# First loads by k-tile, the end in smaller parts, and a smaller stock in the gated embedding

## The chip, the cores and the metric

The kernel runs on one core of a Trainium2 chip. The metric is the device time of one execution in microseconds (us). A core has several engines that run side by side and wait for each other through semaphores: TensorE (PE, matmuls, with its weight loads shown as PEld), VectorE (DVE), ScalarE (ACT), GpSimd (POOL) and SyncE (SP, which here only issues DMAs). Each engine takes its instructions in the order in which the program gives them, so an instruction that waits holds up everything behind it on its engine.

## The reference, cut to what matters

A trunk of two layers over 256 tokens with a model width of 1024. Each layer is half a SwiGLU FFN, a token mixer (latent attention in layer 0, forgetting attention in layer 1), a second half FFN, and a gated embedding. One RMSNorm ends it.

```python
    h = x
    for i in range(DEPTH):
        h = h + 0.5 * swiglu(rms_norm(h, ffn_norm[i, 0]), ffn_w_in[i, 0], ffn_w_out[i, 0])
        u = rms_norm(h, mix_norm[i])
...
        h = h + 0.5 * swiglu(rms_norm(h, ffn_norm[i, 1]), ffn_w_in[i, 1], ffn_w_out[i, 1])
        gate = jax.nn.sigmoid(rms_norm(h, ple_norm[i]) @ ple_w_gate[i])
        h = h + gate * (p[i] @ ple_w_proj[i])
    return rms_norm(h, final_norm)
```

All arrays are float32. The hidden width of the FFN is 2816.

## The kernel before

**Two-part numbers.** Every large matmul is done in the type fp32r on numbers split into a high part and a low part: high x high, low x high, high x low. For the weights, ACT writes the high part `whi` (a copy that rounds, line 98) and DVE the low part `wlo` (raw minus high, line 102). For the activations, `Norm.high` (line 269) multiplies by the gain on ACT, or on DVE where `vector=True`, and `Norm.low` (line 277) makes the rest on DVE. `part` (line 225) runs one k-tile of 128 rows: one matmul with `whi` against both parts of the activations (512 columns), one with `wlo` against the high part (256 columns).

**The stream of weights.** All weights stand in one list, `plan`, in order of use, in blocks of 128 x 1024 (512 KB). `Weights` keeps counters over it: `fetched` (DMA issued on SP into one of four `raw` buffers), `begun` (high part issued on ACT), `loaded` (low part issued on DVE) and `got` (handed to matmuls). `pump` issues high parts up to two blocks ahead, then the low part of one block, and then the next fetches. Each of these is written into the engines' order at the place where `pump` is called. `catch_up(n)` pumps one block if fewer than `n` blocks are loaded beyond `got`. `get` pumps until what it hands out is loaded.

**The start.** `xT` holds the gains (80 columns) and the residual stream by k-tile (8 x 256 columns); it goes into `state` in three pieces, alternating on SP's queue with four slabs of 128 x 1024 that hold, two k-tiles each, the weights of the first two chunks' gate and up (`ffn_first`). Two raw blocks, the tokens `xt` (for the sums of squares by token) and two further raw blocks follow. 22 matmuls on zeros warm up TensorE. Then, per k-tile, ACT and DVE make the pairs of stream and weights, and `first` runs the four products (gate and up of chunks 0 and 1) side by side, k-tile by k-tile.

**The FFN** (line 322). For each of 22 chunks of 128 hidden units, `pg` (gate) and `pu` (up) are made in PSUM from eight k-tiles each. There are seven PSUM banks under the tag "mm", taken in turn. A product leaves its bank when DVE multiplies it by `rb2` (`two`, line 329), the norm's factor per token; that factor comes from `by_token` (`v` on DVE, `rtok` on POOL) and `by_column` (`pb` on PE, `rb` on ACT), which the program issues after the first chunk that follows the waiting ones. Until `rb` is there, no bank is freed. In FFNs other than the first, `blocks` (line 253) runs the first chunk: seven k-tiles of `pg`, seven of `pu`, then the eighth of each.

**The gated embedding of layer 0**, `ple` (line 784). Two blocks of `ple_proj` and then eight of `ple_gate`, one per row d of 128 features. For each d, `gated` issues on DVE the product with `rb` (`zg`), the low part of row d-1's next norm, then weight work (`W.pump(2 - d)` for d under 2, `W.catch_up(3)` for d from 2 to 6), then the product with the gate (`ge`), and the sum into `state`. For the last row it issues `nxt.last` (high and low part on DVE) and then `W.pump()`. The next FFN's first chunk follows.

**The end**, `ple_by_token` (line 827), works with tokens on the partitions (two halves t of 128 tokens). PE makes 512 output columns for both halves, then the other 512: for t = 0 in one piece, for t = 1 in two pieces of 256. After each piece `gated` applies the sigmoid (ACT), the product and the sum (DVE), the square with its sum by token (ACT) and the product with the final gain (DVE). `store` adds the sums, takes the power -1/2 on POOL, scales, and issues the stores. The first store stands between the two last pieces.

## Time and profile before

| | us |
|---|---|
| median of 3 runs | 1001.46 |
| lowest, highest | 1001.19, 1002.36 |
| the profiled execution's own time | 1001.46 |
| its span (first to last instruction) | 999.7 |
| mean granted TensorE clock | 0.998 |

How to read the rows that follow below: a row of the timeline has the start in us from the span's start, the duration, engine, line of the kernel, operation, output <- inputs, shapes, and a count where equal neighbours are merged; in square brackets stands the idle time of that engine before the instruction, and what ended it. A row of a stretch has busy time of each engine with the number of instructions, then the granted clock, the share of the 16 DMA engines, and GB/s.

### The profile page before, as it was taken

What the parts mean: (1) busy time and instruction counts of PE and PEld (TensorE: products, weight loads), DVE (VectorE), ACT (ScalarE), POOL (GpSimd) and SP (SyncE); (2) the same over time, 40 slices, a digit from 0 to 9 for tenths busy, and PEclk for the clock granted to TensorE, in tenths of its full rate; (3) what the DMA queues carried; (4) which work ended last, traced back from release to release, by engine and by line L of the source; (5) the groups of instructions that cost most, each with busy time, mean ns of one, the idle gap of its engine ahead of it and who ended that gap; (6) DMA issues with size and microseconds to landing.
All of it is one profiled execution on the core that took longest, in us unless ns stands there. A gap on an engine that the chain in (4) does not pass through costs nothing.

```text
span 999.7 us, 16018 instructions
## 1 busy us (share of the span) xinstructions
PE 988.8 (99%) x5940; PEld 875.1 (88%) x5940; DVE 740.5 (74%) x1051; ACT 517.6 (52%) x825; POOL 423.7 (42%) x348
## 2 busy tenths in 40 slices
PE   9999999999999999999999999999999999999996
PEld 7888888998988888889888888899889888888886
DVE  5777879676768787667778876666777778876674
ACT  7555444456655544555555444546445554544552
POOL 0777730110267775111477673211221577671120
PEclk9999999999999999999999999999999999999999
DMA  8566666651456666665366656666443566666561
GB/s 330 177 209 208 190 181 191 187 169 53 132 182 207 189 190 185 193 196 195 127 198 206 192 182 192 180 194 206 151 142 102 189 202 199 189 179 201 178 210 43
DMA packets 51388, 180.54 MB, mean 181 GB/s; under 512 B 5872, under 2 KB 6000, under 8 KB 51312
## 3 DMA queue, kind: packets, MB, share of 16 engines
q1 hardware_dynamic: 50880, 178.75, 57.3%
q8 instruction: 47, 0.77, 0.3%
q10 hardware_dynamic: 432, 0.79, 0.3%
q14 instruction: 29, 0.24, 0.1%
HBM read 178.46 MB, written 1.05 MB: 180 GB/s over the span
## 4 chain that ended last, share of the span: by engine, by line
PE 91%; DVE 4%; ACT 2%; issue 1%; POOL 0%; DMA 0%; POOLq 0%; SPq 0%; ACTq 0%; DVEq 0%
PE pu L236 16%; PE po L236 16%; PE pg L236 16%; PE po L237 8%; PE pu L237 8%; PE pg L237 8%; PE ps L236 4%; PE ps L237 2%; DVE wlo L102 1%; PE ps L221 1%; PE ps L223 1%; PE ps L222 1%; PE pv L221 1%; PE pv L223 1%; PE pv L222 1%
## 5 line engine op out<-in xcount | busy, mean ns | idle before, releaser
L102 DVE TENSOR_TENSOR wlo<-raw,whi 128x1024 fp32r<-128x1024 f32 (+2 forms) x338 | 416.8, 1241 | 17.8 <-ACT whi L98 17.1
L98 ACT ACTIVATE whi<-raw 128x1024 fp32r<-128x1024 f32 (+2 forms) x338 | 336.4, 1027 | 20.9 <-DMA raw<-in_ffn_in_dram 12.9
L331 POOL TENSOR_TENSOR gu<-two 128x256 f32<-128x256 f32 x176 | 235.5, 1339 | 117.9 <-DVE two L329 108.4
L236 PE MATMUL pg<-u,whi 128*128 128x512 f32 x704 | 251.7, 395 | 0.8 <-ACT whi L98 0.4
L236 PE MATMUL pu<-u,whi 128*128 128x512 f32 x704 | 251.1, 395 | 0.0
L236 PE MATMUL po<-hs,whi 128*128 128x512 f32 x704 | 246.0, 394 | 0.0
L237 PE MATMUL pg<-u,wlo 128*128 128x256 f32 x704 | 198.2, 282 | 0.3 <-DVE wlo L102 0.2
L237 PE MATMUL po<-hs,wlo 128*128 128x256 f32 x704 | 198.1, 281 | 0.0
L237 PE MATMUL pu<-u,wlo 128*128 128x256 f32 x704 | 198.0, 281 | 0.0
L236 PEld LDWEIGHTS pg<-u,whi 128*128 128x128 f32 x704 | 132.2, 188 | 32.1 <-DVE u L280 1.3
L236 PEld LDWEIGHTS pu<-u,whi 128*128 128x128 f32 x704 | 132.2, 188 | 30.3
L236 PEld LDWEIGHTS po<-hs,whi 128*128 128x128 f32 x704 | 132.2, 188 | 30.2
L237 PEld LDWEIGHTS pg<-u,wlo 128*128 128x128 f32 x704 | 132.5, 188 | 0.9 <-DVE wlo L102 0.9
L237 PEld LDWEIGHTS pu<-u,wlo 128*128 128x128 f32 x704 | 132.5, 188 | 0.0
L237 PEld LDWEIGHTS po<-hs,wlo 128*128 128x128 f32 x704 | 132.5, 188 | 0.0
L291 POOL TENSOR_TENSOR acc<-acc,sq 128x256 f32<-128x256 f32 x42 | 46.0, 1094 | 173.7 <-ACT sq L286 173.5
L213 ACT ACTIVATE hs<-hid 128x256 fp32r<-128x256 f32 x88 | 36.8, 418 | 142.1 <-POOL hid L349 140.1
L349 POOL TENSOR_TENSOR hid<-sg,gu 128x256 f32<-128x256 f32 x88 | 105.2, 1196 | 7.0 <-POOL gu L331 0.2
L217 DVE TENSOR_TENSOR hs<-hid,hs 128x256 fp32r<-128x256 f32 x88 | 63.5, 721 | 48.6 <-ACT hs L213 48.6
L329 DVE TENSOR_TENSOR two<-pg,rb 128x512 f32<-128x512 f32 x88 | 60.3, 685 | 46.8 <-PE pg L237 38.9
L275 ACT ACTIVATE u<-state 128x256 fp32r<-128x256 f32 x57 | 29.0, 509 | 125.7 <-DVE state L392 104.3
L343 ACT ACTIVATE sg<-gu 128x256 f32<-128x256 f32 x88 | 36.8, 418 | 78.5 <-POOL gu L331 78.5
(247 smaller groups left out, 1189.2 us busy)
## 6 DMA issues: line engine op xcount, KB each, us to landing
raw<-in_ffn_in_dram SPq DMA_DIRECT2D x172, 512.0 KB, 4.1
raw<-in_ffn_out_dram SPq DMA_DIRECT2D x64, 512.0 KB, 3.6
raw<-in_ffn_out_dram SPq DMA_DIRECT2D x32, 384.0 KB, 3.7
raw<-in_fox_qk_dram SPq DMA_DIRECT2D x16, 512.0 KB, 3.5
raw<-in_mla_o_dram SPq DMA_DIRECT2D x8, 512.0 KB, 4.4
raw<-in_ple_gate_dram SPq DMA_DIRECT2D x8, 512.0 KB, 4.6
raw<-in_fox_o_dram SPq DMA_DIRECT2D x8, 512.0 KB, 3.7
raw<-in_ple_rows_dram SPq DMA_DIRECT2D x8, 512.0 KB, 4.7
```

What stands on the lines that cost most here:

```text
L98: self.nc.scalar.activation(self.pairs[i][0][:, c], self.raws[i][:, c], AF.Copy)
L102: self.nc.vector.tensor_sub(lo[:, c], self.raws[i][:, c], hi[:, c].bitcast(F32))
L213: nc.scalar.activation(hi, src, AF.Copy)
L217: nc.vector.tensor_sub(lo, src, hi.bitcast(F32))
L236: nc.tensor.matmul(ps, hi, x[:, k], start=k == 0, stop=False)
L237: nc.tensor.matmul(ps[:, 1, :], lo, x[:, k, 0, :], start=False, stop=k == last)
L275: nc.scalar.activation(self.pair[:, b, 0, c], src[:, c], AF.Copy, scale=g)
L291: nc.gpsimd.tensor_add(new, self.acc, sq)
L329: nc.vector.tensor_mul(two, ps, norm.rb2)
L331: nc.gpsimd.tensor_add(gu[c, i], two[:, 0, :], two[:, 1, :])
L343: nc.scalar.activation(sg, gu.pop((c, 0)), AF.Silu)
L349: nc.gpsimd.tensor_mul(hid[c], gu.pop((c, 0)), gu.pop((c, 1)))
```

## The change

Three places are changed.

1. *The start.* The residual stream and the first weights of one k-tile now stand in one row of DRAM per partition, 256 + 512 columns; the row of k-tile 0 has the first 16 gains ahead of it. Eight DMAs bring them. `state`, whole, is loaded by one further DMA behind the tokens and the first raw blocks. The first norm reads its gains from the lead tile and takes its stream from there. The high part of k-tile 0 is made on DVE, there are 18 warm-up matmuls, and for k-tile 0 the four matmuls with high weights come ahead of the four with low ones.
2. *The gated embedding.* `W.catch_up(2)` in place of `W.catch_up(3)` for d from 2 to 6.
3. *The end.* The last 512 columns of token half 1 are made in pieces of 256, 128 and 128, all issued on PE in one go. The sum of squares is carried along piece by piece (`mean`) instead of being reduced at the end; the product with the final gain (`weigh`) is issued apart from the rest; the last scaling is cut into 384 columns on ACT and 640 on DVE, each with its own store.

```diff
@@ -79,10 +79,9 @@
         self.fetched += 1
         return raw, src

-    def take(self, raws):
-
-        self.raws.update(enumerate(raws))
-        self.fetched = self.ahead = len(raws)
+    def skip(self, n):
+
+        self.fetched = self.ahead = n

     def fetch(self):
         while self.fetched < min(len(self.plan), max(self.ahead, self.loaded) + self.RAW):
...
@@ -155,7 +154,7 @@

     def plan_ffn(i):

-        plan.extend(ffn_first[k] for k in range(0 if i else KD // 2))
+        plan.extend(ffn_in[0, c] for c in range(0 if i else KD // 2))
         plan.extend(ffn_in[i, c] for c in range(0 if i else 4, 2 * KF))
         for d in range(KD):
             plan.extend(ffn_out[i, d, :, a * P:min(a + KD, KF) * P] for a in range(0, KF, KD))
@@ -262,12 +261,13 @@
     class Norm:


-        def __init__(self, gain, blocks, dim, tag="u"):
-            self.gain, self.dim, self.acc, self.sums = gain, dim, None, None
+        def __init__(self, gain, blocks, dim, tag="u", table=g_sb):
+            self.g = table[:, gain:gain + blocks]
+            self.dim, self.acc, self.sums = dim, None, None
             self.pair = act.tile([P, blocks, 2, T], F32R, name=tag, bufs=2 if tag == "u" else 1)

         def high(self, b, src, vector=False, cuts=(slice(0, T),)):
-            g = g_sb[:, self.gain + b:self.gain + b + 1]
+            g = self.g[:, b:b + 1]
             for c in cuts:
                 if vector:
                     nc.vector.tensor_scalar(self.pair[:, b, 0, c], src[:, c], g, None, op0=ALU.mult)
...
@@ -793,7 +793,7 @@
             if d < 2:
                 W.pump(2 - d)
             elif d < KD - 1:
-                W.catch_up(3)
+                W.catch_up(2)
             nc.vector.tensor_mul(ge, e, sg)
             nc.vector.tensor_add(src, src, ge)
             if d < KD - 1:
@@ -831,7 +831,7 @@
         nc.sync.dma_start(gain, gain_row.to_broadcast([P, D]))
         N = D // 2
         half = [slice(0, N), slice(N, D)]
-        sums = work.tile([P, 2, 3], F32, name="sums", bufs=1)
+        sums = work.tile([P, 2, 4], F32, name="sums", bufs=1)

         def rows(ps, w, x, k, a, t, last):

@@ -844,21 +844,29 @@
             nc.vector.tensor_mul(sg, es[:, t, a], sg)
             nc.vector.tensor_add(h[:, t, a], h[:, t, a], sg)
             nc.scalar.activation(sg, h[:, t, a], AF.Square, accum_out=sums[:, t, i:i + 1])
+
+        def weigh(t, a):
             nc.vector.tensor_mul(es[:, t, a], h[:, t, a], gain[:, a])

-        def store(t, n):
-            s = work.tile([P, 1], F32, name="s")
-            v = work.tile([P, 1], F32, name="v1")
-            r = work.tile([P, 1], F32, name="r")
-            nc.vector.reduce_sum(s, sums[:, t, :n], axis=AX.X)
-            nc.vector.tensor_scalar(v, s, 1.0 / D, EPS, op0=ALU.mult, op1=ALU.add)
-            nc.gpsimd.tensor_tensor(r, v, mhalf[:, :1], op=ALU.pow)
-            for i, a in enumerate(half):
-                if t and i == 0:
-                    nc.scalar.activation(h[:, t, a], es[:, t, a], AF.Copy, scale=r)
+        def mean(t, i):
+
+            v = work.tile([P, 1], F32, name="v1", bufs=4)
+            nc.vector.tensor_scalar(v, sums[:, t, i:i + 1], 1.0 / D, means[t], op0=ALU.mult, op1=ALU.add)
+            means[t] = v
+
+        def store(t, cuts):
+            for i, (eng, a) in enumerate(cuts):
+                if eng is nc.scalar:
+                    nc.scalar.activation(h[:, t, a], es[:, t, a], AF.Copy, scale=rs[t])
                 else:
-                    nc.vector.tensor_scalar(h[:, t, a], es[:, t, a], r, None, op0=ALU.mult)
-                (nc.scalar if t and i == 0 else nc.sync).dma_start(out[t * P:(t + 1) * P, a], h[:, t, a])
+                    nc.vector.tensor_scalar(h[:, t, a], es[:, t, a], rs[t], None, op0=ALU.mult)
+                (nc.scalar if t and eng is nc.scalar else nc.sync).dma_start(out[t * P:(t + 1) * P, a], h[:, t, a])
+
+        def root(t):
+            rs[t] = work.tile([P, 1], F32, name="r")
+            nc.gpsimd.tensor_tensor(rs[t], means[t], mhalf[:, :1], op=ALU.pow)
+
+        means, rs = {0: EPS, 1: EPS}, {}


         for c in range(2):
@@ -894,64 +902,85 @@
         ws = W.get(KD // 2)
         for t in range(2):
             gated(t, ps[t], half[0], 0)
-        for t in range(2):
-
-            cuts = [half[1]] if t == 0 else [slice(N, N + N // 2), slice(N + N // 2, D)]
-            for i, a in enumerate(cuts):
-                last = bank("ps", (P, a.stop - a.start))
-                for k in range(KD):
-                    b = (k % 2 - 1) * N
-                    rows(last, ws[k // 2], norm.pair, k, slice(a.start + b, a.stop + b), t, KD - 1)
-                gated(t, last, a, 1 + i)
-                if (t, i) == (1, 0):
-                    store(0, 2)
-        store(1, 3)
+            weigh(t, half[0])
+            mean(t, 0)
+
+        cuts = [(0, N, D), (1, N, N + T), (1, N + T, N + T + P), (1, N + T + P, D)]
+        lasts = []
+        for i, (t, a, b) in enumerate(cuts):
+            lasts.append(bank("ps", (P, b - a)))
+            for k in range(KD):
+                o = (k % 2 - 1) * N
+                rows(lasts[i], ws[k // 2], norm.pair, k, slice(a + o, b + o), t, KD - 1)
+        cuts = [(t, slice(a, b)) for t, a, b in cuts]
+        gated(0, lasts[0], half[1], 1)
+        weigh(0, half[1])
+        mean(0, 1)
+        root(0)
+        gated(1, lasts[1], cuts[1][1], 1)
+        store(0, [(nc.vector, a) for a in half])
+        mean(1, 1)
+        gated(1, lasts[2], cuts[2][1], 2)
+        weigh(1, cuts[1][1])
+        mean(1, 2)
+        gated(1, lasts[3], cuts[3][1], 3)
+        weigh(1, slice(N + T, D))
+        mean(1, 3)
+        root(1)
+        c = N - P
+        store(1, [(nc.scalar, slice(0, c)), (nc.vector, slice(c, D))])
         W.done(*ws)


-    n0 = Norm(G_FFN, KD, D)
-    slabs = big.tile([P, KD // 2 + 2, D], F32, name="slabs", tag="big")
-    tokens = slabs[:, KD // 2:, :]
-    W.take([slabs[:, i, :] for i in range(KD // 2)])
-
-    a = 0
-    for i, n in enumerate((2, 2, 4, 0)):
-        if n:
-            b = GAINS + (2, 4, 8)[i] * T
-            nc.sync.dma_start(state[:, a:b], xT[:, a:b])
-            a = b
-        nc.sync.dma_start(slabs[:, i, :], ffn_first[i])
+
+    ROW = T + 4 * P
+    lead = big.tile([P, 2 * KD + KD * ROW + 2 * D], F32, name="lead", tag="big")
+    tokens = lead[:, 2 * KD + KD * ROW:].rearrange("p (t d) -> p t d", t=2)
+    steps = lead[:, 2 * KD:2 * KD + KD * ROW].rearrange("p (k n) -> p k n", k=KD)
+    W.skip(KD // 2)
+    nc.sync.dma_start(lead[:, :2 * KD + ROW], lead0)
+    for k in range(1, KD):
+        nc.sync.dma_start(steps[:, k, :], lead1[k - 1])
     for t in range(2):
         nc.sync.dma_start(*W.raw())
     for t in range(2):
         nc.sync.dma_start(tokens[:, t, :], xt[t])
     W.fetch()
+    nc.sync.dma_start(state, xT)
+    n0 = Norm(G_FFN, KD, D, table=lead)

     warm = const.tile([P, T], BF16, name="warm")
     nc.vector.memset(warm, 0.0)
     cold = bank("cold", (P, T))
-    for _ in range(22):
+    for _ in range(18):
         nc.tensor.matmul(cold, warm[:, :P], warm, start=True, stop=True)
-    half = [slice(0, 4 * P), slice(4 * P, 8 * P)]
     for k in range(KD):
         if k % 2 == 0:
-            W.pair()
-        n0.high(k, hT[:, k, :])
-        W.high(k // 2, half[k % 2])
-        n0.low(k, hT[:, k, :])
-        W.low(k // 2, half[k % 2])
+            hi, lo = W.pair()
+        c = slice(k % 2 * 4 * P, (k % 2 + 1) * 4 * P)
+        n0.high(k, steps[:, k, :T], vector=k == 0)
+        nc.scalar.activation(hi[:, c], steps[:, k, T:], AF.Copy)
+        n0.low(k, steps[:, k, :T])
+        rest(hi[:, c], lo[:, c], steps[:, k, T:])
         if k % 2:
             W.loaded += 1

     def first(ps):
-        for k in range(0, KD, 2):
-            w, = W.get()
-            for j in range(2):
-                for i, p in enumerate(ps):
-                    part(p, w, n0.pair, range(k + j, k + j + 1), KD - 1, at=lambda x: (j * 4 + i) * P)
-            W.done(w)
-            W.pump()
-            if k == 0:
+        w, = W.get()
+
+        for i, p in enumerate(ps):
+            nc.tensor.matmul(p, w[1][:, i * P:(i + 1) * P], n0.pair[:, 0], start=True, stop=False)
+        for i, p in enumerate(ps):
+            nc.tensor.matmul(p[:, 1, :], w[2][:, i * P:(i + 1) * P], n0.pair[:, 0, 0, :], start=False, stop=False)
+        for k in range(1, KD):
+            if k % 2 == 0:
+                w, = W.get()
+            for i, p in enumerate(ps):
+                part(p, w, n0.pair, range(k, k + 1), KD - 1, at=lambda x: (k % 2 * 4 + i) * P)
+            if k % 2:
+                W.done(w)
+                W.pump()
+            if k == 1:

                 n0.sums = const.tile([P, 2], F32, name="sums")
                 for t in range(2):
@@ -1114,9 +1143,10 @@

     w = ffn_w_in.reshape(4, KD, P, 2, KF, P)

-    a["ffn_first"] = np.ascontiguousarray(
-        w[0, :, :, :, :2].transpose(0, 1, 3, 2, 4).reshape(KD // 2, 2, P, 4 * P).transpose(0, 2, 1, 3)).reshape(
-            KD // 2, P, D)
+    lead = w[0, :, :, :, :2].transpose(0, 1, 3, 2, 4).reshape(KD, P, 4 * P)
+    lead = np.concatenate([xT.reshape(P, KD, T).transpose(1, 0, 2), lead], axis=2)
+    a["lead0"] = np.ascontiguousarray(np.concatenate([g[:, :2 * KD], lead[0]], axis=1))
+    a["lead1"] = np.ascontiguousarray(lead[1:])
     a["ffn_in"] = np.ascontiguousarray(w.transpose(0, 4, 3, 2, 1, 5)).reshape(4, 2 * KF, P, KD * P)
     w = ffn_w_out.reshape(4, KF, P, KD, P)
     a["ffn_out"] = np.ascontiguousarray(w.transpose(0, 3, 2, 1, 4)).reshape(4, KD, P, KF * P)
```

More of the change, by code (lines that the diff above doesn't have):

```diff
@@ L141, in trunk @@
 @with_exitstack
-def trunk(ctx, tc, xT, xt, pT, pos, freq, bf, ffn_first, ffn_in, ffn_out, w_down, w_uq, w_ukv, mla_o,
+def trunk(ctx, tc, xT, xt, pT, pos, freq, bf, lead0, lead1, ffn_in, ffn_out, w_down, w_uq, w_ukv, mla_o,
           fox_qk, fox_v, fox_f, fox_o, ple_gate, ple_proj, ple_rows, gain_row, out):
@@ L277, in low @@
         def low(self, b, src, cuts=(slice(0, T),)):
-            g = g_sb[:, self.gain + b:self.gain + b + 1]
+            g = self.g[:, b:b + 1]
             for c in cuts:
@@ L1154, in _layout @@
     return a
-_ORDER = ["xT", "xt", "pT", "pos", "freq", "bf", "ffn_first", "ffn_in", "ffn_out", "w_down", "w_uq", "w_ukv", "mla_o",
+_ORDER = ["xT", "xt", "pT", "pos", "freq", "bf", "lead0", "lead1", "ffn_in", "ffn_out", "w_down", "w_uq", "w_ukv", "mla_o",
           "fox_qk", "fox_v", "fox_f", "fox_o", "ple_gate", "ple_proj",
```

## The prediction

> **What bounds the kernel now.** I read the summary of engines, then the chain of work that ended last, then TensorE's waits.
>
> ```profile
> PE 988.8 (99%) x5940; PEld 875.1 (88%) x5940; DVE 740.5 (74%) x1051; ACT 517.6 (52%) x825; POOL 423.7 (42%) x348
> PE 91%; DVE 4%; ACT 2%; issue 1%; POOL 0%; DMA 0%; POOLq 0%; SPq 0%; ACTq 0%; DVEq 0%
> 942.08 0.24 PE po L236
> ```
>
> TensorE (PE) is busy for 99% of the span and is 91% of the chain. The third row is one step of that chain in order of time: a 512-column matmul holds PE for 0.24. So an edit counts in three places only: before PE's stream begins, after it ends, and where PE stands still. Time that PE loses anywhere is not won back later, because nothing after it has slack; time saved on another engine counts only where PE waits for it. The profiled execution took 1001.46 us, which is also the median; its span is 999.7, so 1.76 lie around it. All terms below are differences to this execution.
>
> **The start.** First the rows of the first k-tile, from the timeline.
>
> ```profile
> 1.08 4.87 PE L934 MATMUL cold<-warm 128*128 128x256 bf16 x22 [1.08 <-DVE warm L931]
> 3.59 0.51 ACT L275 ACTIVATE u<-state 128x256 fp32r<-128x256 f32 x1 [1.36 <-DMA state<-in_xT_dram]
> 4.13 0.48 DVE L280 SCALAR_TENSOR_TENSOR u<-state,u 128x256 fp32r<-128x256 f32 x1 [3.10 <-ACT u L275]
> 5.66 0.63 ACT L98 ACTIVATE whi<-slabs 128x512 fp32r<-128x512 f32 x1 [1.57 <-DMA slabs<-in_ffn_first_dram]
> 7.07 0.39 PE L237 MATMUL pg<-u,wlo 128*128 128x256 f32 x1 [0.23 <-DVE wlo L102]
> 486.37 0.35 DVE L273 TENSOR_SCALAR u<-state 128x256 fp32r<-128x256 f32 x1
> 18.14 0.39 PE L236 MATMUL pg<-u,whi 128*128 128x512 f32 x1
> ```
>
> Before, ScalarE (ACT) waits for the first piece of the stream (592 columns, 303 KB) until 3.59 and for the first slab (827 KB in all) until 5.66. After, one DMA of 784 columns (401 KB) brings gains, stream and weights of k-tile 0; between those two landings it arrives at about 4.0. The weights' high part takes ACT 0.63; beside it VectorE (DVE) makes the stream's pair (0.35 by L273, 0.48 by L280), so PE could begin near 4.9. The warm-up of 18 matmuls instead of 22, 0.22 each, ends at 5.1, which costs nothing, as four high matmuls stand ahead of the first low part. Before, the steady pace begins in effect at 6.84 (7.07, less the one matmul issued ahead of it). So PE is 1.8 us early; but k-tile 1 (393 KB more, 1.55 us by the same two landings) arrives at 5.5, needs 0.51 and 0.63 on ACT and 0.7 on DVE (as from 6.29 to 7.07 before), and PE, done with k-tile 0 at 6.5, loses 0.6. Later k-tiles arrive faster than PE's 1.4 us each. So PE reaches the third chunk (18.14 before) some 1.2 us early. Should its first matmuls still run at the warm-up's pace (0.22 for 256 columns, against 0.118 below), that is up to 1.4 us less, and lies inside the waits that follow. The new order of k-tile 0 adds no matmul, and SP's one issue more runs ahead of the data.
>
> Does that gain last? Next PE needs the norm's factor and then a free PSUM bank.
>
> ```profile
> 14.00:18.00 4.00, 4.00 (x24) 3.50 (x23) 3.58 (x5) 3.99 (x6) 0.00 (x0) 1.00 1.03 420
> 22.03 0.16 DVE L308 TENSOR_SCALAR v<-sums 128x2 f32<-128x2 f32 x1
> 22.34 0.71 POOL L310 TENSOR_TENSOR rtok<-v,mhalf 128x2 f32<-128x2 f32 x1 [20.85 <-DVE v L308]
> 23.75 0.60 PE L315 MATMUL pb<-ident,rtok 128*128 128x128 f32 x4
> 23.33 1.06 ACT L98 ACTIVATE whi<-raw 128x1024 fp32r<-128x1024 f32 x1 [0.17 <-DMA raw<-in_ffn_in_dram]
> 24.39 0.39 ACT L318 ACTIVATE rb<-pb 128x256 f32<-128x256 f32 x1
> 24.81 0.69 DVE L329 TENSOR_TENSOR two<-pg,rb 128x512 f32<-128x512 f32 x1 [0.40 <-ACT rb L318]
> 27.00 0.39 PE L236 MATMUL pu<-u,whi 128*128 128x512 f32 x1
> ```
>
> In the stretch 14 to 18 the DMA engines are full (share 1.03, 420 GB/s). The bytes queued ahead of the weights are the same up to plan entry 7, so `v` at 22.03 and `rtok` until 23.05, which stand behind that entry's split, do not move; PE, arriving 1.2 us early at `pb` (23.75), waits there until 23.1. At most 0.6 of the gain is left.
>
> The second wait is worse. The change reads the residual stream twice: once inside the rows, once more into `state` (1.09 MB), and this second read is queued on SP behind entries 6 and 7 and ahead of entries 8 and 9. The lead rows are 3.15 MB against 3.19 before, so 1.06 MB more stand ahead of entry 9: at 420 GB/s 2.5 us. The trace has no such read, so its delay is bounded: 0 if the queue empties in time, 2.5 if it stays full; I take 2.3, as the queue is full in the nearest row and the early rows may move a little faster than before's. Behind ACT's wait for entry 9 (23.33) stands `rb` on the same engine, behind `rb` the first `two`, and behind `two` the bank that the fourth chunk's `pu` needs: seven banks, of which four hold chunks 0 and 1, two chunk 2 and one the gate of chunk 3. Before, `two` was done at 25.50 and PE came at 27.00, 1.5 us of slack. After, it is done at 27.8, and PE starts `pu` at about 27.9: **+0.9** (bounds -0.6, with no delay, to +1.3). What PE gained at the front it then spends waiting.
>
> **The middle.** `catch_up(2)` for `catch_up(3)` in the gated embedding. Here the count of split weight blocks decides, so I followed it through the rows.
>
> ```profile
> 477.77 1.22 DVE L102 TENSOR_TENSOR wlo<-raw,whi 128x1024 fp32r<-128x1024 f32 x1
> 481.31 1.22 DVE L102 TENSOR_TENSOR wlo<-raw,whi 128x1024 fp32r<-128x1024 f32 x1
> 487.16 4.04 DVE L102 TENSOR_TENSOR wlo<-raw,whi 128x1024 fp32r<-128x1024 f32 x3
> L102 DVE TENSOR_TENSOR wlo<-raw,whi x5: 1214/1218/1769, 477.8 to 490.0; 128x1024 fp32r<-128x1024 f32 x5
> 484.98 0.50 PE L236 MATMUL pg<-u,whi 128*128 128x512 f32 x1 [0.35 <-DVE u L280]
> 485.43 0.40 PE L236 MATMUL pu<-u,whi 128*128 128x512 f32 x1
> 488.98 0.39 PE L237 MATMUL pg<-u,wlo 128*128 128x256 f32 x1
> 489.21 0.39 PE L236 MATMUL pg<-u,whi 128*128 128x512 f32 x1
> 497.76 1.49 DVE L102 TENSOR_TENSOR wlo<-raw,whi 128x1024 fp32r<-128x1024 f32 x1
> 498.12 0.39 PE L236 MATMUL pu<-u,whi 128*128 128x512 f32 x1
> 500.90 0.39 PE L236 MATMUL pg<-u,whi 128*128 128x512 f32 x1
> 501.35 1.21 DVE L102 TENSOR_TENSOR wlo<-raw,whi 128x1024 fp32r<-128x1024 f32 x1
> ```
>
> Number the blocks from the embedding's first. In steps d = 2 to 4 no block is split, in d = 5 (477.77) and d = 6 (481.31) one each, and three follow the last row's norm (487.16). That pattern fits one count only: four blocks in stock at the entry, so these are blocks 10, 11 and then 12, 13, 14. The next FFN's first gate is block 10, its `pu` block 11, its second gate block 12, which in fact waits for its split (488.98 comes 0.19 late). With a stock of two, d = 5 splits none, d = 6 splits block 10, and **block 11 falls behind the last row's norm** on DVE, where block 12 was. But PE wants block 11 before that norm: `pu` runs its first seven k-tiles ahead of the eighth of `pg`.
>
> The saved 1.22 on DVE brings the last norm forward by less: DVE's row 6 waits for PE's row-6 matmuls, so 0.55 to 1.2, I take 0.8. So block 11's split starts at 486.4 instead of 487.16, takes 1.77 as the first of the three did (max 1769), and ends near 488.2. `pu`'s first low part, at 485.67 before, then runs at 488.2: +2.5. The 0.35 wait for `u` at 484.98 goes, but lies inside that; ACT splits two blocks ahead, so the high part is there; the wait at 488.98 goes, about -0.3. The stock stays one short: the slot 497.76 to 499.25, which follows PE's `pb` and moves with PE, now brings the block that PE wants at 498.12 + 0.24, so 0.9 more, and the slot at 501.35 (until 502.56) the one for 500.90 + 0.24, moved by 0.9: 0.5 more. Then VectorE is ahead again. Sum 2.2 + 0.9 + 0.5 = **+3.6** (bounds 2.0, if the later two are absorbed, to 3.9).
>
> **The end.** Of the last 512 columns of token half 1, 256 + 256 become 256 + 128 + 128; the two reductions become sums carried along, and the last scaling is cut 384 (ACT) to 640 (DVE).
>
> ```profile
> 964.46 0.53 PEld L305 LDWEIGHTS pst<-ones,acc 128*128 128x128 f32 x4 [0.16 <-POOL acc L291]
> 967.56 1.90 PEld L879 LDWEIGHTS ph<-ident,state 128*128 128x128 f32 x16
> 986.17 0.28 PE L221 MATMUL ps<-whi,u 128*128 128x256 f32 x1
> 991.74 0.28 PE L223 MATMUL ps<-wlo,u 128*128 128x256 f32 x1
> 992.12 0.47 ACT L843 ACTIVATE sgr<-ps,rtok 128x256 f32<-128x256 f32 x1 [0.97 <-PE ps L223]
> 987.09 0.69 DVE L844 TENSOR_TENSOR sgr<-fin,sgr 128x512 f32<-128x512 f32 x1 [1.92 <-ACT sgr L843]
> 992.78 0.42 DVE L844 TENSOR_TENSOR sgr<-fin,sgr 128x256 f32<-128x256 f32 x1
> 994.23 0.16 DVE L853 TENSOR_REDUCE s<-sums 128x1 f32<-128x3 f32 x1
> 995.24 0.72 ACT L858 ACTIVATE fin<-fin,r 128x512 f32<-128x512 f32 x1 [1.04 <-POOL r L855]
> ```
>
> From 986.17 to 991.74 stand 47 steps: 0.118 each at 256 columns. What a 128-column matmul of this type costs the trace doesn't show. Each has its own weight load, and loads never follow closer than 0.114: 16 in 1.90, so (1.90 - 0.188)/15, and 4 in 0.53 even where one column is streamed. So I take 0.114: 48 small matmuls are 5.5 us where 24 of 256 took 2.8, **+2.65**. Bounds: 0.059, the columns alone, and 0.18, plain f32, by `pb` (four loads in the 0.36 from 23.75). Behind it, the tail from 992.12: sigmoid, product, sum and square shrink by 0.11 to 0.13 each (0.69 against 0.42 on DVE is 0.13 per 128), the reduction (0.16 and its start) goes for 0.19, the last scaling of 384 instead of 512 columns saves 0.14: -0.8. The other edits there (both `weigh`, the order of `store(0)`) lie beside matmuls, since DVE and ACT wait for PE from 990 on. Together **+1.85** (ends -0.8 and +5.0).
>
> The Trainium skill, page "TensorE: Matmul & The Clock Gate", section "Back-to-back issue gap", gives a sustained stream of loads and 128-column matmuls about 81 ns each. By that the 48 would be an estimated 3.9 us and the end +0.3; the trace, at 0.114 for f32 loads, speaks against it.
>
> **Sum.** 0.9 + 3.6 + 1.85 = 6.35, so 1001.46 + 6.35 = 1007.8 us.
>
> **The rivals.** *A, the second read is hidden:* it doesn't delay entry 9, the start ends at -0.6, 1006.3 us. For it: entry 9 waits only 0.17 now. Against: the full queue. Chance 0.12. *B, narrow matmuls at half price:* 0.059 each, the end at -0.8, 1005.2. For it: 256 columns take half of 512. Against: the 0.114. Chance 0.12; the Trainium skill's 81 ns lies between this and the forecast. *C, narrow matmuls dearer:* 0.18 each, 48 x 0.18 - 2.8 = 5.8, less 0.8, 1011.0. For it: every matmul of this type here has 256 columns or more. Chance 0.10. *D, the other side, the middle is covered:* if one block more lies in stock at the embedding's entry (five, not four), block 11 is split before the last norm; then both waits, 0.5 with its refill and 0.3, go: -0.8 for +3.6, so 1003.4, within what a measurement can tell from no change (0.2%, 2.0 us). It decides at the point where block 11's split is done by 484.8. Against: with five, d = 5 would have split none before. Chance 0.10. The forecast keeps 0.56.
>
> **How the numbers follow.** The forecast's own bounds (start 0.4 to 1.3, middle 2.0 to 3.9, end 1.2 to 2.0) give 1005.1 to 1008.7. A and B reach down to about 1004, C up to 1011; D is left out. Range 1003.8 to 1011.0. Faster by over 0.2%: only D together with A or B, 0.04. Within 0.2%: the rest of D and neighbours, 0.12. Slower: 0.84.
>
> **What would show it.** Start: first fp32r matmul near 4.9; then PE waits before the fourth chunk's `pu`, with ACT waiting for `raw` ahead of `rb`. Without these waits, A. Middle: PE idle of 2 to 3 us at the second block of the third FFN, released by `wlo`; none would be D. End: loads of the last two pieces 0.114 apart (0.059: B; 0.18: C), and 0.8 less from the last matmul to the last store. A PE wait elsewhere would mean that I missed a dependency.

## The result, and the profile after

| | us | ratio to before, 95% interval |
|---|---|---|
| before, median of 4 runs | 1001.41 (1001.19 to 1002.36) | |
| after, median of 4 runs | 1009.68 (1009.13 to 1011.0) | 1.0079, 1.0066 to 1.0093 |
| profiled execution before: time, span | 1001.46, 999.7 | |
| profiled execution after: time, span | 1009.13, 1007.3 | |

The change makes the kernel 8.3 us slower; the forecast was 6.35. Busy time and chain of the kernel after, from its page:

```profile
PE 992.4 (99%) x5960; PEld 878.2 (87%) x5960; DVE 742.4 (74%) x1056; ACT 517.9 (51%) x827; POOL 424.6 (42%) x348
...
PE 88%; DVE 5%; ACT 3%; issue 2%; DMA 2%; POOL 1%; SPq 0%; POOLq 0%; ACTq 0%; DVEq 0%
```

PE still bounds the kernel: its busy time grew by 3.6 us, the span by 7.6. The other 4.0 us are idle time of PE. The view of waits of the kernel after (engine, waiting instruction, what released it, total us, times, longest) says where most of it is:

```profile
PE pu L236 <- DVE wlo L101: 3.9, 2, 3.1
...
PE pu L235 <- DVE two L329: 0.7, 1, 0.7
...
PE pb L315 <- POOL rtok L310: 0.4, 1, 0.4
```

None of these three stands in this list of the kernel before, which goes down to waits of 0.2; what else is left in the two lists is nearly the same. To split the rest by stage I use two marks that lie behind the first and the second change: the matmuls `pe` near 453 (after the whole first half of the program, ahead of the gated embedding) and the last `pst` near 965 (ahead of the end). The view of a tile gives first and last start; before first, then after:

```profile
L221 PE MATMUL pe<-q,whi x16: 278/282/368, 452.8 to 459.2; 128*128 128x256 f32 x16
...
L305 PE MATMUL pst<-ones,acc x32: 164/250/271, 197.7 to 964.8; 128*128 128x1 f32 x32
```

```profile
L220 PE MATMUL pe<-q,whi x16: 278/282/368, 453.1 to 459.5; 128*128 128x256 f32 x16
...
L305 PE MATMUL pst<-ones,acc x32: 166/250/271, 198.1 to 970.7; 128*128 128x1 f32 x32
```

| | forecast | profiled execution |
|---|---|---|
| start: `pe`, 452.8 to 453.1 | +0.9 | +0.3 |
| middle: `pe` to last `pst`, 512.0 to 517.6 | +3.6 | +5.6 |
| end: last `pst` to the span's end, 34.9 to 36.6 | +1.85 | +1.7 |
| sum | +6.35 | +7.6 |

The marks are rounded to 0.1 us, and so are these differences. Every comparison by stage below is of one profiled execution with another; the medians are of all executions.

**The start after**, from the timeline:

```profile
1.08 3.52 PE L956 MATMUL cold<-warm 128*128 128x256 bf16 x18 [1.08 <-DVE warm L953]
5.02 0.47 PE L972 MATMUL pg<-u,whi 128*128 128x512 f32 x1 [0.42 <-DVE u L280]
...
22.21 0.71 POOL L310 TENSOR_TENSOR rtok<-v,mhalf 128x2 f32<-128x2 f32 x1 [20.72 <-DVE v L308]
...
22.97 0.71 PE L315 MATMUL pb<-ident,rtok 128*128 128x128 f32 x4 [0.36 <-POOL rtok L310]
...
25.10 1.06 ACT L97 ACTIVATE whi<-raw 128x1024 fp32r<-128x1024 f32 x1 [0.18 <-DMA raw<-in_ffn_in_dram]
26.06 0.36 ACT L318 ACTIVATE rb<-pb 128x256 f32<-128x256 f32 x1
...
27.21 0.50 PE L235 MATMUL pu<-u,whi 128*128 128x512 f32 x1 [0.73 <-DVE two L329]
```

PE's first product begins at 5.02 instead of 6.34 (the prediction reckoned from 6.84, where the steady pace of before in effect begins), and PE reaches `pb` at 22.97 instead of 23.75. The row of before:

```profile
6.34 0.50 PE L236 MATMUL pg<-u,whi 128*128 128x512 f32 x1 [0.39 <-ACT whi L98]
```

Then the making of the high part of plan entry 9 starts at 25.10 (23.33 before), `rb` behind it at 26.06 (24.39 before), and the fourth chunk's `pu` has to wait for its bank: 27.21 against 27.00. The early start is gone.

**The middle after**, timeline and then stretches (busy time and count of PE, PEld, DVE, ACT, POOL; granted clock; DMA share; GB/s):

```profile
486.37 0.48 DVE L280 SCALAR_TENSOR_TENSOR u<-state,u 128x256 fp32r<-128x256 f32 x1
486.77 4.02 DVE L101 TENSOR_TENSOR wlo<-raw,whi 128x1024 fp32r<-128x1024 f32 x3
...
488.57 0.55 PE L236 MATMUL pu<-u,wlo 128*128 128x256 f32 x1 [3.07 <-DVE wlo L101]
488.92 0.63 PE L235 MATMUL pu<-u,whi 128*128 128x512 f32 x1
489.35 0.41 PE L236 MATMUL pu<-u,wlo 128*128 128x256 f32 x1
...
503.62 0.39 PE L236 MATMUL pu<-u,wlo 128*128 128x256 f32 x1 [0.79 <-DVE wlo L101]
...
506.93 0.39 PE L236 MATMUL pg<-u,wlo 128*128 128x256 f32 x1 [0.22 <-DVE wlo L101]
```

```profile
485.22:488.63 3.41, 0.34 (x3) 0.06 (x1) 3.31 (x6) 2.59 (x4) 0.84 (x1) 1.00 0.01 5
488.63:492.04 3.41, 3.41 (x11) 2.93 (x12) 2.16 (x2) 0.66 (x1) 0.00 (x0) 0.50 0.67 202
```

The low part of block 11 is made behind the last row's norm, as forecast, and PE stands still for 3.07. What I had not looked for is the second row: the granted clock is 0.50 for 3.41 us after that wait, and in it a matmul of 512 columns holds PE for 0.43 (488.92 to 489.35) where 0.24 is normal. At half speed those 3.41 us hold 1.7 us of normal work.

**The end after**, timeline:

```profile
994.77 0.28 PE L222 MATMUL ps<-wlo,u 128*128 128x256 f32 x1
994.88 0.22 PE L220 MATMUL ps<-whi,u 128*128 128x128 f32 x1
994.94 0.27 PE L221 MATMUL ps<-whi,u 128*128 128x128 f32 x1
995.05 0.28 PE L222 MATMUL ps<-wlo,u 128*128 128x128 f32 x1
...
1000.08 0.27 PE L222 MATMUL ps<-wlo,u 128*128 128x128 f32 x1
```

The 48 narrow matmuls start 5.20 / 47 = 0.111 apart. Only the first is followed after 0.06 (994.88 to 994.94). The rows of the weight loads show why:

```profile
994.77 0.19 PEld L220 LDWEIGHTS ps<-whi,u 128*128 128x128 f32 x1
994.89 0.19 PEld L221 LDWEIGHTS ps<-whi,u 128*128 128x128 f32 x1
995.00 0.19 PEld L222 LDWEIGHTS ps<-wlo,u 128*128 128x128 f32 x1
```

The loads keep starting 0.11 to 0.12 apart all the time. The first narrow matmul starts 0.11 after its load, behind the last wide one; the second starts 0.05 after its load and the third 0.05 after its own, so from there on the pace is that of the loads. From the last of them to the span's end it is 7.2 (1007.3 - 1000.08), where it was 8.0 before (999.7 - 991.74).

### The profile page after: what moved, and what is told of

It is laid out like the page before. It is cut to its first block, busy times and chain, and to the rows that moved or that the text cites. A ratio compares the mean times of both kernels' runs of the same rounds, so it can differ in the third digit from the quotient of the medians.

```text
span 1007.3 us, 16069 instructions
## 1 busy us (share of the span) xinstructions
PE 992.4 (99%) x5960; PEld 878.2 (87%) x5960; DVE 742.4 (74%) x1056; ACT 517.9 (51%) x827; POOL 424.6 (42%) x348
## 4 chain that ended last, share of the span: by engine, by line
PE 88%; DVE 5%; ACT 3%; issue 2%; DMA 2%; POOL 1%; SPq 0%; POOLq 0%; ACTq 0%; DVEq 0%
PE po L235 16%; PE pu L235 16%; PE pg L235 15%; PE po L236 8%; PE pu L236 8%; PE pg L236 8%; PE ps L235 4%; PE ps L236 2%; DMA raw<-in_ffn_in_dram 2%; DVE wlo L101 2%; PE ps L220 1%; PE ps L222 1%; PE ps L221 1%; PE pv L220 1%; PE pv L222 1%
## 5 line engine op out<-in xcount | busy, mean ns | idle before, releaser
L275 ACT ACTIVATE u<-state 128x256 fp32r<-128x256 f32 x49 | 25.0, 510 | 123.8 <-DVE state L392 103.6
## 6 DMA issues: line engine op xcount, KB each, us to landing
raw<-in_ffn_in_dram SPq DMA_DIRECT2D x172, 512.0 KB, 4.0
raw<-in_ffn_out_dram SPq DMA_DIRECT2D x64, 512.0 KB, 3.6
raw<-in_fox_qk_dram SPq DMA_DIRECT2D x16, 512.0 KB, 3.6
raw<-in_mla_o_dram SPq DMA_DIRECT2D x8, 512.0 KB, 4.0
raw<-in_ple_gate_dram SPq DMA_DIRECT2D x8, 512.0 KB, 4.5
raw<-in_fox_o_dram SPq DMA_DIRECT2D x8, 512.0 KB, 3.5
raw<-in_ple_rows_dram SPq DMA_DIRECT2D x8, 512.0 KB, 5.0
```

The lines of the kernel that those rows point to most:

```text
L275: nc.scalar.activation(self.pair[:, b, 0, c], src[:, c], AF.Copy, scale=g)
```

## The experiments

Theory: three prices that add up (a bank wait in the start from the second read, a late low part with a clock drop in the middle, narrow matmuls in the end). Rivals: A, B, C and D of the prediction; for the middle, that the clock drop is an accident of one execution; for the start, that something other than the second read holds it back. Each kernel is compared with the kernel before on the same chip. The medians of before were 1001.57 for the kernels of the first comparison (`m_only`, `e_only`, `s_only`, `s_late`), 1001.87 for those of the second (`m_fill`, `e_256`, `a_c3`, `s_early`), and 1001.39 for the last three (`a_again`, `a_fill`, `s_early_e256`).

**One part alone.** Three kernels, each the kernel before with one of the three parts of the change. The middle alone is one line:

```diff
-                W.catch_up(3)
+                W.catch_up(2)
```

> The kernel before with the middle's edit alone (a stock of two instead of three). Theory: block 11's low part falls behind the last row's norm, so TensorE stands still for about 3 us ahead of the next FFN's first up product, runs at half clock for some 3.4 us after it (1.6 us lost), and waits about 1.0 us more for the two following blocks; the two waits of before (0.35 and 0.3) go. Sum +5.6: 1007.0 us. Rival, the middle costs only when the start is moved as well: under 1003.

> The kernel before with the end's edit alone (256, 128, 128 columns; sums carried along). Theory: 48 matmuls of 128 columns at 0.11 us in place of 24 of 256 at 0.118 add 2.5 us, the tail behind the last matmul is 0.7 shorter: +1.8, 1003.2 us. Rival, the narrow pieces cost nothing by themselves and the profiled difference is noise between executions: within 0.3 of 1001.4.

> The kernel before with the start's edit alone. Theory: TensorE begins 1.8 us earlier, loses it at the norm's factor (about 0.4) and at the bank that waits for the factor behind the ninth weight block (0.7), and is 0.3 behind from there: 1001.7 us. Rival, the first matmuls' lead lasts: 1000.2.

| | median, us | ratio, 95% interval |
|---|---|---|
| m_only, the middle alone | 1006.81 | 1.0048, 1.0034 to 1.0062 |
| e_only, the end alone | 1004.84 | 1.003, 1.0019 to 1.0042 |
| s_only, the start alone | 1002.46 | 1.0004, 0.9995 to 1.0013 |

The middle costs most, the end next, the start little. The middle alone is as expected (1007.0), the start alone 0.8 above its 1001.7. The end alone came out 1.6 us above what I expected, and the timeline of its profiled execution shows two things that the profile of before doesn't have:

```profile
23.09 1.23 DVE L102 TENSOR_TENSOR wlo<-raw,whi 128x1024 fp32r<-128x1024 f32 x1
...
23.30 1.59 POOL L310 TENSOR_TENSOR rtok<-v,mhalf 128x2 f32<-128x2 f32 x1 [21.81 <-DVE v L308]
...
24.94 0.71 PE L315 MATMUL pb<-ident,rtok 128*128 128x128 f32 x4 [1.63 <-POOL rtok L310]
...
995.54 0.27 PE L223 MATMUL ps<-wlo,u 128*128 128x128 f32 x1
```

This is the kernel before's own start, and yet `rtok` on POOL took 1.59 here and 0.71 in the profile shown of before, because DVE's split, begun just before, ran beside it; PE waited 1.63 for it. The old start has both kinds of execution: `pb` waited 1.29 in the profile of m_only, 1.43 in that of m_fill, and not at all in those of before and e_256. That is probably why the runs of the kernel before lie near 1001.2 or near 1003.0, and it makes the median of before one between two groups: a difference under 1 us from it tells little. The wait is not of the end's making. The last narrow matmul starts 3.8 later than before's last (991.74): 1.3 of that comes from this start, the rest from the narrow matmuls. In the end itself the last store took 3.5 from issue to landing in this execution, against 2.5 before and 2.6 in the six other profiles with a store of this size (view of DMA issues: kind, size, us):

```profile
out_dram<-fin ACTq DMA_DIRECT2D x1, 192.0 KB, 3.5
```

How much of this the other executions of e_only had, and so how the 1.6 of the median comes about, is not shown.

**The end in wider parts.** The end of the change with two parts of 256 columns in place of 256, 128 and 128; all else of the new end is kept.

```diff
-        cuts = [(0, N, D), (1, N, N + T), (1, N + T, N + T + P), (1, N + T + P, D)]
+        cuts = [(0, N, D), (1, N, N + T), (1, N + T, D)]
...
```

> The end's edit with the last 256 columns in one piece (256, 256 instead of 256, 128, 128), all else of the end kept. Theory: the price is in the narrow matmuls; here the tail alone is shorter (no reduction 0.2, last scaling 0.14): 0.3 under before, 1001.2 us. Rival, the order of the end's work or its last stores of 384 and 640 columns cost something too: 1002 or more.

1001.62, ratio 0.9996 (0.9987 to 1.0005): no difference that can be measured. Without the narrow matmuls the new end costs nothing that can be measured. In its timeline the last matmul starts at

```profile
991.98 0.28 PE L223 MATMUL ps<-wlo,u 128*128 128x256 f32 x1
```

and the span ends at 999.7, 7.7 later. So the price of the end is the 48 narrow matmuls (48 x 0.111 = 5.3 us where 24 of 256 columns took 2.8: +2.5), of which only 0.7 comes back behind them.

**The middle undone.** The changed kernel with the stock of three blocks.

```diff
-                W.catch_up(2)
+                W.catch_up(3)
```

> The changed kernel with the middle undone (stock of three). Theory: the parts add up, so start (+0.9 as measured alone) and end (+3.3 as measured alone) remain: 1005.7 us, and no wait for a weight block's low part in the third FFN but the 0.35 and 0.3 of before. Rival, the start's extra read keeps the end or the middle out of another loss: under 1004.

1003.9 (1003.68 to 1004.88), ratio 1.0018 (1.0009 to 1.0027), 1.8 us under what I expected, and just where the rival said: under 1004. What the parts cost alone does not add up: e_only's 3.3 holds the wait for `rtok` of the old start (and, in its profile, the late store), and with the new start neither was there (`rtok` took 0.71 in a_c3, the last store 2.6). The middle is worth 1009.68 - 1003.9 = 5.8 us in the changed kernel by the two medians, or 6.2 if each is first compared with before on its own chip (8.3 and 2.0); start and end together cost some 2.0. Two waits of its list:

```profile
PE pu L235 <- DVE two L329: 1.6, 1, 1.6
...
PE pg L235 <- DVE u L280: 0.9, 1, 0.9
```

and its marks:

```profile
L220 PE MATMUL pe<-q,whi x16: 278/282/367, 453.5 to 459.9; 128*128 128x256 f32 x16
...
L305 PE MATMUL pst<-ones,acc x32: 164/250/271, 198.6 to 966.1; 128*128 128x1 f32 x32
```

The wait for `wlo` is gone. The middle is 966.1 - 453.5 = 512.6, 0.6 above before, with a wait of 0.9 for `u` where there was 0.35. The same stretch is 512.4 in s_only, s_late and s_early, with waits for `u` of 0.7, so this small rest comes with the new start and not with its second read. Why the embedding's VectorE work falls that much behind there, I have not found out.

**The wait filled.** Is the half clock a consequence of PE's idle time? 24 matmuls of zeros, written to a spare bank, are put between the two products of the first chunk of the third FFN. They don't shorten the wait; they only keep PE active through it. First on the kernel before with the stock of two, then on the changed kernel, which was run again beside it.

```diff
                 part(p, w, x, ks, KD - 1)
+                if fill and p is ps[0] and ks[0] == 0:
+                    spare = psm.tile([P, T], F32, name="spare", tag="small")
+                    for _ in range(fill):
+                        nc.tensor.matmul(spare, warm[:, :P], warm, start=True, stop=True)
...
```

> The middle's edit alone, with 24 matmuls on zeros (256 columns, bf16, 0.11 us each) put into TensorE's stand-still ahead of the up product. Theory: in some executions the idle stretch of about 3 us drops the clock to a half for 3.4 us, which costs 1.6; the filling keeps it, and changes nothing of the wait itself: clock 1.0 behind the stall in the profile, no run above 1007.5, median 1005.3 to 1006.8. Rival, the half clock has nothing to do with the idle stretch: as the middle's edit alone, 1005.5 to 1008.8, with the drop still to be seen.

> The changed kernel as it is, as the base of the next run: about 1009.7 us by the first comparison. Its wait for the low part of block 11 is 3.07 us long in the profiled execution, and the granted clock reads half for 3.41 us after it. If the half clock is no accident of that one execution, this profile has it again.

> The changed kernel with 24 matmuls of zeros (256 columns, bf16) put on PE into the wait for block 11's low part; the output is unchanged. Theory (the idle time itself pulls the granted clock down to a half, which adds about 1.6 us to a wait that stays as long as it was): no half clock after the wait, and 1009.7 - 1.6 = about 1008.1 us. Rival (the half clock has another cause, or falls in few executions only): the same time as the changed kernel, about 1009.7 us, or slower if the filling outlasts the wait (24 matmuls took 2.79 us in the earlier run of this filling, the wait is 3.07).

| | median, us | ratio, 95% interval |
|---|---|---|
| m_fill (m_only filled) | 1005.51 | 1.0034, 1.0022 to 1.0047 |
| a_again (the changed kernel) | 1009.31 | 1.0082, 1.0068 to 1.0096 |
| a_fill (the changed kernel filled) | 1007.5 | 1.0062, 1.0049 to 1.0075 |

m_fill lies within the expected 1005.3 to 1006.8, a_fill 0.6 under its expected 1008.1. Doing 24 useless matmuls makes the changed kernel 1.8 us faster by the medians. The two intervals overlap a little, so the profiles and the granted clocks of the single executions have to carry it. The changed kernel again, timeline, then the stretch of the half clock and the one ahead of it:

```profile
489.58 0.38 PE L236 MATMUL pu<-u,wlo 128*128 128x256 f32 x1 [3.04 <-DVE wlo L101]
```

```profile
490.36:493.78 3.42, 3.42 (x12) 2.89 (x11) 1.43 (x2) 0.69 (x1) 0.00 (x0) 0.50 0.86 277
486.95:490.36 3.41, 0.78 (x4) 0.73 (x5) 3.34 (x4) 3.26 (x4) 0.84 (x1) 1.00 0.00 0
```

The half clock is there again, again for 3.41 us. The filled kernel, timeline, a stretch and its marks:

```profile
485.29 2.79 PE L261 MATMUL spare<-warm 128*128 128x256 bf16 x24
488.75 0.39 PE L236 MATMUL pu<-u,wlo 128*128 128x256 f32 x1 [0.43 <-DVE wlo L101]
```

```profile
490.00:492.00 2.00, 2.00 (x14) 1.75 (x13) 0.96 (x1) 0.00 (x0) 0.00 (x0) 1.00 0.82 299
```

```profile
L220 PE MATMUL pe<-q,whi x16: 278/282/368, 453.3 to 459.7; 128*128 128x256 f32 x16
...
L309 PE MATMUL pst<-ones,acc x32: 166/250/272, 198.3 to 969.3; 128*128 128x1 f32 x32
```

Block 11's low part comes as late as ever (488.75), but the clock stays at 1.00, and the middle is 969.3 - 453.3 = 516.0 instead of 517.6 in both profiles of the changed kernel (a_again: 454.1 and 971.7). So of the middle's 5.6 us, 1.6 are the clock and 4.0 the wait with its refilling and the waits behind it.

The mean granted clock that is on record for every execution says the same. None of the 66 executions of before beside these kernels lies under 0.996, and none of the ten filled ones under 0.997. Of the changed kernel's ten (after and a_again), five do: 0.995 at 1009.34, 1010.03 and 1010.1 us, 0.994 at 1011.0, 0.992 at 1013.09. The one at 0.998 took 1007.33, as little as the filled kernel (1007.39 to 1008.26). a_again's profile, with one drop, has 0.995; so the executions at 0.994 and 0.992 probably had more than one, which no trace shows.

The pair on the kernel before shows less. In m_only's profile the wait was 2.89 and no clock drop followed it (timeline, then two stretches):

```profile
489.52 0.39 PE L237 MATMUL pu<-u,wlo 128*128 128x256 f32 x1 [2.89 <-DVE wlo L102]
```

```profile
484.79:488.20 3.41, 1.84 (x11) 1.33 (x9) 2.96 (x6) 2.01 (x5) 1.39 (x2) 1.00 0.47 144
488.20:491.62 3.42, 2.10 (x12) 1.86 (x13) 3.42 (x3) 2.05 (x3) 0.18 (x1) 1.00 0.28 86
```

Its middle is 515.9 (454.2 to 970.1), the same as m_fill's (454.0 to 969.9). So a wait of this length does not bring the drop in every execution. Of m_only's five, the slowest, 1008.78, has a mean clock of 0.995, so some have it; but the 1.3 us between the two medians can also come from the old start's two kinds of execution, and five of each don't tell them apart.

What decides is where the wait lies in time. In all thirteen traces every change of the granted clock lies a whole number of times 3.4133 us behind the first entry of the clock's record, which itself stands anywhere from 3.94 to 7.07 us after the span's start: 142 and 143 times for the half clock in both profiles of the changed kernel, 290 to 293 for the fall after each kernel's last matmul. So time is cut into windows of 3.4133 us that the kernel doesn't set. In the changed kernel the half clock followed windows in which PE was busy for 0.34 and 0.78. In m_only the wait lies across a border at 488.20: the two rows above are the two windows, with PE busy for 1.84 and 2.10, and the clock stays. At the kernel's end it fell after a window with 1.41 (m_fill, 995.69 to 999.10) and not after one with 1.73 (s_early, 989.46 to 992.87). So the limit lies between 1.4 and 1.7 us of work in a window, as far as these traces go; narrow matmuls seem to count for less, as e_only's clock fell after a window with 1.90.

The Trainium skill, page "TensorE: Matmul & The Clock Gate", section "What's actually happening", says that the clock is halved after an idle window of about 3.4 us, that the window is 3413 ns long, and that it runs freely and doesn't reset when a kernel starts. The length agrees: the half clock lasted 3.41 us twice. The free running agrees too, by the multiples of 3.4133 us, and it explains why 2.89 us went without a drop. That a whole window must be idle does not agree: PE was busy for 0.34 us of the window ahead of the drop in the one profile and 0.78 in the other.

**The second read moved.** The start alone, with the read into `state` issued behind the four leading products; then the same with the first norm's factor (`by_token`) issued after the third pair of k-tiles of the leading products instead of after the next chunk's gate.

```diff
     W.fetch()
-    nc.sync.dma_start(state, xT)
...
+        nc.sync.dma_start(state, xT)
```

```diff
             if k % 2:
                 W.done(w)
                 W.pump()
+            if k == 5:
+                n0.by_token()
...
-                norm.by_token()
+                if not first:
+                    norm.by_token()
```

> The start's edit alone, with the second read of the residual stream issued only after the first FFN's leading products, behind four more weight blocks. Theory: the second read ahead of blocks 8 and 9 is what delays the factor; without it the wait for the bank goes, the wait for the factor itself stays, and TensorE is about 0.6 ahead of before from there on: 1000.8 us. Rival, the delay comes from the shape or the rate of the leading rows: same as the start's edit alone, 1001.7.

> The start's edit with the late second read, and the first norm's factor made 2 us sooner (its instructions issued after the third pair of k-tiles instead of after the next chunk's gate), so that GpSimd's power doesn't run beside VectorE's split of the next weight block. Theory: in the runs with the late read the power took 1.6 to 1.8 beside that split and 0.71 without it, and TensorE waited 1.1 for it; now neither wait is left, TensorE keeps its lead of 1.2: 1000.2 us. Rival, the power is slow for a reason of its own: 1001.4, with the wait at the factor still there.

s_late came out at 1001.43, ratio 0.9995 (0.9986 to 1.0004), s_early at 1000.75, ratio 0.9985 (0.9976 to 0.9994). Each lies between what I expected (1000.8, 1000.2) and its rival (1001.7, 1001.4). In s_only PE waits for `two`, as in the changed kernel (timeline):

```profile
27.60 0.50 PE L235 MATMUL pu<-u,whi 128*128 128x512 f32 x1 [0.94 <-DVE two L329]
```

In s_late that wait is gone, so the second read was its cause. But another takes its place in the profiled execution, which at 1002.57 is one of the longest of its eleven (the shortest took 1000.89, about the 1000.8 expected; timeline of s_late):

```profile
22.53 1.22 DVE L101 TENSOR_TENSOR wlo<-raw,whi 128x1024 fp32r<-128x1024 f32 x1
...
22.55 1.77 POOL L310 TENSOR_TENSOR rtok<-v,mhalf 128x2 f32<-128x2 f32 x1 [21.06 <-DVE v L308]
...
24.38 0.71 PE L315 MATMUL pb<-ident,rtok 128*128 128x128 f32 x4 [1.08 <-POOL rtok L310]
```

With the read out of the way, plan entry 8 lands earlier, DVE splits it just when POOL takes the power, and `rtok` needs 1.77. In both runs with the collision `rtok` ends 0.57 after DVE's instruction (22.55 + 1.77 = 24.32 against 23.75; in e_only 24.89 against 24.32). The same holds for every `rtok` in all thirteen traces, ten in each: where a split had begun before it, it took 1.54 to 1.77 and ended 0.55 to 0.57 after the split; in all other cases it took 0.71, also where a split began 0.2 after it (before, 198.50 and 198.70). The Trainium skill, page "SBUF — State Buffer", section "SBUF: two separate sides", describes this: VectorE (with two inputs in SBUF) and GpSimd share a pair of ports by an exclusive lock; whichever starts first holds it for the whole instruction, and the other waits. These times agree with it. s_early does not avoid the collision, against what I had expected (`rtok` takes 1.68 there), but puts it where PE does not wait yet (timeline of s_early; `pb` follows at 22.58 without a wait for it):

```profile
20.85 1.68 POOL L310 TENSOR_TENSOR rtok<-v,mhalf 128x2 f32<-128x2 f32 x1 [19.37 <-DVE v L308]
```

**Both good parts together.** s_early's start, e_256's end, the stock of three.

> Two parts that each held against the kernel before, put together: the start by k-tile with the second read late and the first norm's factor early (1000.75 us alone, 1.1 under the kernel before in its batch), the end with two parts of 256 columns (0.25 under the kernel before), the stock of three blocks kept. Theory (start and end do not meet, so they add): 1000.75 - 0.25 = 1000.5 us, 0.13 to 0.14 per cent under the kernel before. Rival (the end's gain is the chance landing time of one store): 1000.75 us or above.

1000.49 (1000.34 to 1001.23), ratio 0.999 (0.9982 to 0.9999). It is the fastest kernel here, by its interval just faster than before, and none of its eleven runs (1000.34 to 1001.23) lies near the 1003 that the kernel before also shows. The expected size came out, but it lies 0.26 under s_early's run, which is too little to tell the end's part from nothing.

## Why the prediction was right or wrong

**The bound.** Right: PE's stream has no slack. The marks divide the span, so the three differences must add up to its difference; what bears the forecast out is that the list of PE's waits has grown in these places alone.

**The start, +0.9 forecast.** The mechanism was right in each step: the early first matmul (4.9 forecast, 5.02 found), the wait at `pb` until 23.1, ACT waiting for entry 9 with `rb` behind it, the bank as the last wait. One term was too large for this execution: the second read delayed entry 9 by 1.8, not 2.3, so PE came to `pu` at 27.21 instead of 27.9, and the start cost 0.3. In other executions of the same start entry 9 came later (by the ACT rows, 2.1 in a_fill, 2.2 in s_only, 2.3 in a_c3, 2.9 in a_again, the last above the bound of 2.5) and the wait was longer (1.6 in a_c3 and in a_again, whose `pe` marks are 453.5 and 454.1, +0.7 and +1.3). s_only's median is +0.9; in its profile +0.7 stands at `pe` and +0.4 in the middle (512.4). The upper bound of +1.3 was not worked out rightly: a delay of 2.5 gives +1.1. A is refuted by s_only's and a_c3's wait for `two`, and s_late names the cause. What I missed altogether: `rtok` has two durations, and the old start sometimes pays 1.3 to 1.6 for it, which the second read happens to prevent (0.71 in all five profiles with the early second read). I priced it from a single row of 0.71.

**The middle, +3.6 forecast, +5.6 found.** This is the step that was too small. The count of blocks was right: in the row x3 at 486.77 block 11 stands behind the last norm, and the low part ran at 488.57, less the 0.3 of the start 488.3, forecast 488.2. The later waits of 0.9 and 0.5 were 0.79 and 0.22. The lower bound, without these two, should have been 2.2 and not 2.0. The sum had no term for the clock: 1.6 us by a_fill, which leaves 4.0 against 3.6. I had quoted a row of the granted clock but never asked what a wait of 3 us would do to it. The rest of 0.4 I have not split; the refilling of PE after each wait (0.39 for a matmul that shows 0.28 in the stream) may be a part of it. D is refuted by the wait of 3.07, and its count was wrong as I put it: with a stock of two at the rows d = 5 and 6, it would have taken six blocks at the entry, not five, to have block 11 ready.

**The end, +1.85 forecast, +1.7 found.** Right, term by term: 0.111 between narrow matmuls (0.114 forecast, +2.5 for +2.65), 0.7 less behind the last one (0.8 forecast). B (0.059) and C (0.18) are refuted by that row, and so is, for this type at least, the 81 ns that the Trainium skill, page "TensorE: Matmul & The Clock Gate", section "Back-to-back issue gap", states for such a stream. The pace is that of loads with a single column behind them in the prediction's rows (0.114), so the load seems to set it; that the loads go on 0.11 apart, whether the matmul behind them has 256 columns or 128, says the same. Loads without matmuls were not run. e_256 shows that the narrow parts are the end's whole price, as far as its interval can tell.

**The sum.** 1007.8 forecast, 1009.68 found. In the profiled execution (1009.13) the start came out 0.6 under its term, the middle 2.0 over it and the end about right: the start's error hid part of the missing clock term, and that the total came so near owes something to luck. The median lies 0.55 above that execution, as other executions had a later entry 9 or, by their mean clocks, more time at half clock.

## What to carry to other kernels

Where a change makes the bounding engine wait, price not only the wait: if it can leave TensorE less than about 1.5 us of work in 3.4, add the 1.6 us that the halved clock cost here, as a price that some executions pay and others don't. If the wait can't go, a few matmuls of zeros in it are cheaper than silence. A matmul of this type cut from 256 to 128 columns costs nearly as much as before (0.111 for 0.118), so count the weight loads, not the columns, before work at the end is cut finer. Before a transfer is added to a full queue, follow which instruction waits for the entries behind it, and what stands in line behind that instruction on its engine.

## What the hardware showed beyond what I expected

- PE's granted clock fell to 0.50 for 3.41 us in both profiles of the changed kernel, after waits of 3.07 and 3.04 us; the drop came at once in the one (488.63, PE resumed at 488.57) and 0.78 after the resumption in the other (490.36, 489.58). After a wait of 2.89 in m_only there was none; the changes of the clock lie on a grid of 3.4133 us, and that wait lay across one of its borders.
- A power of 128 x 2 numbers on POOL took 0.71, and 1.54 to 1.77 where a split on VectorE had begun before it, ending 0.55 to 0.57 after that instruction. A split that began after the power left it at 0.71.
- The last store of 192 KB took 3.5 us to land in e_only; the 256 KB of before took 2.5, and 192 KB took 2.6 in six other profiles. A fetch of instructions began 1.9 after the store's issue in e_only, and more than 4.1 after it in those six and in before; that it was the cause was not tried.
